# A hybrid RWKV-7 decoder block: the recurrence in chunks of 64 with all chunks batched, in place of chunks of 128 one after another

## The chip, the core and the metric

The kernel runs on one core of a Trainium2 chip. The metric is device time in microseconds (us) of one launch. Work is spread over engines that run their own instruction streams in a fixed order and meet at semaphores: TensorE (PE, matrix products into PSUM), VectorE (DVE), ScalarE (ACT), GpSimd (POOL) and SyncE (SP), whose queue issues most loads and stores.

## The reference

One decoder block over 512 tokens, width 2048, all in float32. What the change touches is the RWKV-7 mixer: 16 heads of 64 channels, each with a 64x64 state that runs through the 512 tokens.

```python
def _wkv7_scan(r, w, k, v, a, b):
    def step(S, inp):
        r_t, w_t, k_t, v_t, a_t, b_t = inp
        sa = jnp.einsum('bhvk,bhk->bhv', S, a_t)
        S = S * w_t[:, :, None, :] + sa[..., None] * b_t[:, :, None, :] + v_t[..., None] * k_t[:, :, None, :]
        y = jnp.einsum('bhvk,bhk->bhv', S, r_t)
        return S, y
...
    y = _wkv7_scan(r_h, decay, k_h, v_h, -kk, kk * a_h)
    # group norm of y per head, + bonus, * gate
...
    mix = jnp.concatenate([y_rwkv, y_pool], axis=-1) @ w_out[l]
    x = x + gt1 * mix
    x = x + gt2 * _conv_ffn(h, w_up[l], conv_w[l], conv_b[l], w_down[l])
```

Ahead of the scan stand the adaLN product, an RMS norm and the input projection `w_in`; beside it a causal pooling mixer; behind it the output projection and a gated MLP with a causal convolution of width 3.

## The kernel before

Activations lie channels by tokens, 128 channels on the partitions. Large products run in float32r with weights and activations split into a high and a low part, three matmuls each (`mm3`, L120 to L122); the recurrence's small products are plain float32.

The heads are handled as eight pairs, two heads on 128 partitions. For each pair:

- `stage_a` (L366) makes decay, key, value and the keys `bt`, `kt`, the queries `ar` (a removal part and a reading part), the scores of `bt` against the removal part (L417, masked at L420 into `nt`), and inverts the 16x16 diagonal blocks of (I - nt), through DRAM, on DVE (L435, L437). It ends with the bonus `bv`.
- `stage_b` (L466) doubles the inverse: from 16 to 32 with 32x32 products (L474, L483), from 32 to 64 (L496 to L508), and from 64 to 128 (L514 to L519). The result is `y1`, `y2`.
- `stage_c` (L523) walks through four chunks of 128 tokens, one after another. Each chunk transposes v, bt and kt (L532, copied by ACT at L534), makes three blocks of scores (L539, L541) and masks them (L542), multiplies the state and the values into R (L547, L550, copied at L553), applies the inverse (L556, L557, copied at L559 as U), forms the next state `sbd` (L562, L564, L573) and three sums of the output y (L578, L580, L582). A group norm with two 128x128 products (L590, L594), the gate (L602, L603) and a store to DRAM follow.

Around it, `win_pair` (21 tiles of input projection, spilled to DRAM) and `ada_rest` (192 adaLN products on DVE at L351, each with a 256 KB load) stand in the program at ordinary priority. The recurrence stands under `hp()`, a high priority. A scheduler orders each engine's stream at build time by priority and by its own estimate of readiness; on the chip the orders are fixed. `stage_c` of one pair is followed by `stage_b` of the next; `stage_a` of the next comes before them.

PSUM has eight banks: two for `mm`, two for `pa`, two joined as `pb`, one `y`, one `ch`.

A matmul with 64 rows contracted or 64 columns of weights occupies a part of the 128x128 array. The trace writes that as rows*columns (64*128, 128*64, 64*64, 32*32).

Of the kernel before, what the change touches and what calls it, by code (L numbers as in the profile page):

```python
# [9 lines left out]
F32 = mybir.dt.float32  # L10
# [6 lines left out]
P = 128  # L17
T = 512
# [4 lines left out]
NC = 4  # L23
WC = 512
# [31 lines left out]
def block_kernel(ctx, tc, a, out, stop=None, dbg=None):  # L56
# [18 lines left out]
    masks = tp.tile([P, 4, P], F32, tag="masks", name="masks")  # L75
    nc.sync.dma_start(masks, a["mask4"][:, :, :])
    mlev = tp.tile([P, 2, 64], F32, tag="mlev", name="mlev")
    nc.sync.dma_start(mlev, a["mlev"][:, :, :])
    scanm = tp.tile([P, NC, 129], F32, tag="scanm", name="scanm")
# [236 lines left out]
    def btile():  # L316

        return psa.tile([P, 2, T], F32, tag="pb", name="pb")

    def ctile(tag):  # L320
        return psa.tile([P, T], F32, tag=tag, name=tag)
# [11 lines left out]
    y1 = ra.tile([P, 8, 64], F32, tag="y1", name="y1")  # L333
    G.memset(y1[64:128], 0.0)
# [22 lines left out]
    def ch(t):  # L357
        return t[:, :].rearrange("p (c t) -> p c t", c=NC)
# [7 lines left out]
    def stage_a(p, rkv):  # L366
# [10 lines left out]
        sg = ra.tile([P, NC, 129], F32, tag="sg", name="sg", bufs=2)  # L377
        V.memset(sg[:, :, 0:1], 0.0)
        S.activation(sg[:, :, 1:129], ch(psw), AF.Sigmoid, bias=col("w0", p))
        al = ring("al")  # L380
        S.activation(al, psal, AF.Sigmoid, bias=col("a0", p))
        cs = ra.tile([P, NC, 129], F32, tag="sg", name="cs", bufs=2)
        V.tensor_tensor_scan(cs[:, :, :].rearrange("p c t -> p (c t)"), scanm[:, :, :].rearrange("p c t -> p (c t)"),
                             sg[:, :, :].rearrange("p c t -> p (c t)"), 0.0, op0=ALU.mult, op1=ALU.add)
        mid = ra.tile([P, NC, 1], F32, tag="mid", name="mid", bufs=2)
        V.tensor_copy(mid, cs[:, :, 64:65])
        V.tensor_sub(cs, cs, mid[:, :, :].to_broadcast([P, NC, 129]))
        ep = ra.tile([P, NC, 129], F32, tag="ep", name="ep")
        S.activation(ep, cs, AF.Exp, scale=-Q)
        em = ra.tile([P, NC, 129], F32, tag="em", name="em")  # L390
        S.activation(em, cs, AF.Exp, scale=Q)
        fdec = q.fdec = ra.tile([P, NC - 1, 1], F32, tag="fdec", name="fdec", bufs=2)
        V.tensor_mul(fdec, ep[:, 0 : NC - 1, 128:129], em[:, 1:NC, 0:1])
# [5 lines left out]
        PE.matmul(psn, bones, sq, start=True, stop=True)  # L399
        inv = ring("inv")  # L400
# [4 lines left out]
        ar = q.ar = ra.tile([P, NC, 2, P], F32, tag="ar", name="ar", bufs=2)  # L405
        V.scalar_tensor_tensor(ar[:, :, 0, :], ch(inv), -1.0, ep[:, :, 0:128], op0=ALU.mult, op1=ALU.mult)
        bt = q.bt = ra.tile([P, T], F32, tag="bt", name="bt", bufs=2)
        V.tensor_mul(bt, inv, al)
        V.tensor_mul(ch(bt), ch(bt), em[:, :, 1:129])
# [9 lines left out]
        for h in range(2):  # L419
            V.tensor_mul(ntv[:, h, :, :], ch(pss[h]), masks[:, 0:1, :].to_broadcast([P, NC, P]))  # L420
# [846 lines left out]
```

## Time and profile before

| | |
|---|---|
| runs | 2365.44, 2365.26, 2360.84 us; median 2365.26 |
| span of the profiled execution | 2365.6 us |
| granted TensorE clock, mean | 0.989 |
| PE busy, over the span | 2259.0 us, 95% |
| DVE, ACT, POOL busy | 1637.7, 1066.4, 126.2 us |
| DMA moved | 483.06 MB, mean 204 GB/s |

The profile is one execution. Busy time is the union of an engine's instructions. A group's row gives line, engine, operation, output and inputs, shapes, count, busy time, mean length of one in ns, idle time ahead of it and what ended that. A float32 matmul shows as two instructions of the same line. Matmuls overlap in their pipeline, and their ends are modelled, so the distance from start to start is what one costs, not its length.

### The profile page before, as it was taken

What the parts mean: (1) busy time and instruction counts of PE and PEld (TensorE: products, weight loads), DVE (VectorE), ACT (ScalarE), POOL (GpSimd) and SP (SyncE); (2) the same over time, 40 slices, a digit from 0 to 9 for tenths busy, and PEclk for the clock granted to TensorE, in tenths of its full rate; (3) what the DMA queues carried; (4) which work ended last, traced back from release to release, by engine and by line L of the source; (5) the groups of instructions that cost most, each with busy time, mean ns of one, the idle gap of its engine ahead of it and who ended that gap; (6) DMA issues with size and microseconds to landing.
All of it is one profiled execution on the core that took longest, in us unless ns stands there. A gap on an engine that the chain in (4) does not pass through costs nothing.

```text
span 2365.6 us, 42857 instructions
## 1 busy us (share of the span) xinstructions
PE 2259.0 (95%) x17122; PEld 1965.8 (83%) x17122; DVE 1637.7 (69%) x2591; ACT 1066.4 (45%) x1499; POOL 126.2 (5%) x185
## 2 busy tenths in 40 slices
PE   3879999999999999999999999999999999999997
PEld 2656666666666789999999999999999888888897
DVE  6987687777684456788888877777777645353354
ACT  3235253445433345665555555555555522233353
POOL 0000000000000000010101000000000000110000
PEclk9999999999999999999999999999999999999999
DMA  9976556566672756598888877777776767663464
GB/s 345 339 232 184 164 157 175 153 179 188 172 207 74 242 190 191 169 284 246 231 245 234 237 212 199 197 198 199 199 197 185 237 212 272 228 211 117 123 183 160
DMA packets 226234, 483.06 MB, mean 204 GB/s; under 512 B 74545, under 2 KB 79601, under 8 KB 217841
## 3 DMA queue, kind: packets, MB, share of 16 engines
q1 hardware_dynamic: 206114, 413.21, 54.5%
q0 software_dynamic: 18864, 66.07, 13.6%
q8 instruction: 134, 2.20, 0.4%
q10 hardware_dynamic: 1056, 1.05, 0.1%
q14 instruction: 66, 0.54, 0.1%
HBM read 441.70 MB, written 38.54 MB: 203 GB/s over the span
## 4 chain that ended last, share of the span: by engine, by line
PE 57%; issue 8%; DVE 1%; DMA 1%; ACT 1%; POOL 0%; POOLq 0%; DVEq 0%; ACTq 0%
PE b L122 18%; PE b L120 18%; PE b L121 18%; DMA wrow<-wup 1%; PE mm L122 1%; PE mm L121 1%; PE mm L120 1%; PE pb L122 0%; PE pa L122 0%; PE pa L120 0%; PE pa L121 0%; PE pb L120 0%; PE pb L121 0%; ACT x L787 0%; PE pa L298 0%
## 5 line engine op out<-in xcount | busy, mean ns | idle before, releaser
L122 PE MATMUL b<-t,ulo 128*128 128x256 f32 x1408 | 397.2, 282 | 0.0
L120 PE MATMUL b<-t,uhi 128*128 128x256 f32 x1408 | 396.8, 282 | 0.0
L121 PE MATMUL b<-t,uhi 128*128 128x256 f32 x1408 | 396.7, 282 | 0.0
L122 PE MATMUL b<-act,ulo 128*128 128x512 f32 (+1 forms) x880 | 308.0, 350 | 0.0
L121 PE MATMUL b<-act,uhi 128*128 128x512 f32 (+1 forms) x880 | 307.8, 350 | 0.0
L120 PE MATMUL b<-act,uhi 128*128 128x512 f32 (+1 forms) x880 | 307.7, 350 | 0.0
L120 PE MATMUL b<-y,uhi 128*128 128x256 f32 x1056 | 297.4, 282 | 2.7 <-ACT uhi L854 2.7
L122 PE MATMUL b<-y,ulo 128*128 128x256 f32 x1056 | 297.3, 282 | 0.5 <-DVE ulo L856 0.5
L121 PE MATMUL b<-y,uhi 128*128 128x256 f32 x1056 | 297.1, 281 | 0.0
L856 DVE TENSOR_TENSOR ulo<-wd,uhi 128x1024 fp32r<-128x1024 f32 (+1 forms) x120 | 136.3, 1136 | 217.9 <-ACT uhi L854 213.0
L113 ACT CAST whi<-wraw 128x512 fp32r<-128x512 f32 x236 | 145.5, 620 | 274.7 <-PE mm L121 115.3
L120 PEld LDWEIGHTS b<-t,uhi 128*128 128x128 f32 x1408 | 266.9, 190 | 0.0
L122 PEld LDWEIGHTS b<-t,ulo 128*128 128x128 f32 x1408 | 266.9, 190 | 0.0
L121 PEld LDWEIGHTS b<-t,uhi 128*128 128x128 f32 x1408 | 266.8, 190 | 0.0
L854 ACT CAST uhi<-wquart 128x1024 fp32r<-128x1024 f32 x156 | 164.0, 1052 | 202.6 <-PE b L121 176.2
L854 ACT CAST uhi<-wd 128x1024 fp32r<-128x1024 f32 (+1 forms) x120 | 117.6, 980 | 293.2 <-PE b L121 291.1
L856 DVE TENSOR_TENSOR ulo<-wquart,uhi 128x1024 fp32r<-128x1024 f32 x156 | 190.9, 1224 | 72.0 <-ACT uhi L854 72.0
L115 DVE TENSOR_TENSOR wlo<-wraw,whi 128x512 fp32r<-128x512 f32 x236 | 161.1, 688 | 100.3 <-ACT whi L113 92.6
L854 ACT CAST uhi<-r 128x1024 fp32r<-128x1024 f32 x132 | 138.8, 1051 | 163.2 <-PE b L121 161.3
L856 DVE TENSOR_TENSOR ulo<-r,uhi 128x1024 fp32r<-128x1024 f32 x132 | 161.3, 1222 | 61.9 <-ACT uhi L854 61.9
L120 PEld LDWEIGHTS b<-y,uhi 128*128 128x128 f32 x1056 | 199.6, 189 | 3.1 <-ACT uhi L854 3.1
L122 PEld LDWEIGHTS b<-y,ulo 128*128 128x128 f32 x1056 | 199.3, 189 | 0.9 <-DVE ulo L856 0.9
(314 smaller groups left out, 4719.0 us busy)
## 6 DMA issues: line engine op xcount, KB each, us to landing
wquart<-wup SPq DMA_DIRECT2D x176, 512.0 KB, 4.8
wa<-ada SPq DMA_DIRECT2D x48, 1024.0 KB, 6.9
war<-ada SPq DMA_DIRECT2D x192, 256.0 KB, 3.4
wd<-wdn SPq DMA_DIRECT2D x80, 512.0 KB, 3.8
wraw<-win SPq DMA_DIRECT2D x140, 256.0 KB, 4.1
wraw<-wout SPq DMA_DIRECT2D x96, 256.0 KB, 3.5
wquart<-wup POOLq DMA_DIRECT2D x44, 512.0 KB, 7.5
r<-wup SPq DMA_DIRECT2D x44, 512.0 KB, 4.6
```

Of the source, the lines that this page charges most:

```text
L113: S.copy(hi, raw)
L115: eng.tensor_tensor(lo, raw, hi[:, :].bitcast(F32), op=ALU.subtract)
L120: PE.matmul(ps, wh, xh, start=start, stop=False, skip_group_check=more)
L121: PE.matmul(ps, wh, xl, start=False, stop=False, skip_group_check=more)
L122: return PE.matmul(ps, wl, xh, start=False, stop=stop, skip_group_check=more)
L854: S.copy(hi[:, 0:n], src)
L856: lo_of[0] = V.tensor_tensor(lo[:, 0:n], src, hi[:, 0:n].bitcast(F32), op=ALU.subtract)
```

## The change

The recurrence runs in eight chunks of 64 tokens. The two chunks of a former chunk of 128 lie on the two halves of the partitions (index e), the two heads on the two halves of the channels (index h). The inverse is doubled up to 64 only. All products of a pair that need no state are made for all eight chunks together: scores, W = T A and U0 = T L V, the transition matrix `gd` of each chunk, the state's input, and the parts of the output that need no state. Six steps then carry the state from chunk to chunk, each a 128x128 by 128x64 matmul and one DVE operation that scales and adds; fourteen products with the states complete the output. The PSUM banks `y` and `ch` become one double tile `py`; the group norm and the gate use `pa`. The mask table shrinks from four 128x128 masks to two of 128x64. The remaining lines of the diff change sizes and names alike.

```diff
+L = 64
+NL = T // L
...
-    masks = tp.tile([P, 4, P], F32, tag="masks", name="masks")
+    masks = tp.tile([P, 2, L], F32, tag="masks", name="masks")
...
-    sbd = [ra.tile([P, P], F32, tag=f"sbd{i}", name=f"sbd{i}") for i in range(2)]
-    for t in sbd:
-        G.memset(t, 0.0)
+    gd = ra.tile([P, NL, P], F32, tag="gd", name="gd")
+    G.memset(gd, 0.0)
...
+        sb = q.sb = ra.tile([P, 8, 3, L], F32, tag="sb", name="sb", bufs=2)
         pss = [atile() for h in range(2)]
-        for c in range(NC):
-            for h in range(2):
-                PE.matmul(pss[h][:, c * P : (c + 1) * P], bt[HS[h], c * P : (c + 1) * P], ar[HS[h], c, 0, :],
-                          start=True, stop=True)
+        scores([pss[h] for h in range(2)], bt, ar)
...
+    def scores(banks, keys, ar):
+        for c in range(NC):
+            for e in range(2):
+                for h in range(2):
+                    j = 2 * c + e
+                    PE.matmul(banks[h][HS[e], c * 2 * L : (c + 1) * 2 * L], keys[HS[h], jl(j)], ar[HS[h], :, j, :],
+                              start=True, stop=True)
...
+    def to_rows(src, dst, eng):
+        ps = atile()
+        for c in range(NC):
+            PE.transpose(ps[:, c * P : (c + 1) * P], src(c), ident)
+        eng(dst, ps[:, :].rearrange("p (c h d) -> p h c d", c=NC, h=2))
...
     def stage_b(p, q):
+        pk = btile()
+        scores([pk[:, h, :] for h in range(2)], kt, ar)
+        V.tensor_mul(sk, pk[:, :, :].rearrange("p h (c i t) -> p (h c) i t", c=NC, i=2),
+                     masks[:, None, :, :].to_broadcast([P, 8, 2, L]))
+        to_rows(lambda c: v[:, c * P : (c + 1) * P], by_head(tok[:, 0, :, :]), S.copy)
+        to_rows(lambda c: ar[:, 0, 2 * c : 2 * c + 2, :].rearrange("p e t -> p (e t)"), by_head(rw[:, :, 0, :]), S.copy)
+        to_rows(lambda c: bt[:, c * P : (c + 1) * P], by_head(sb[:, :, 2, :]), S.copy)
+        to_rows(lambda c: kt[:, c * P : (c + 1) * P], by_head(tok[:, 1, :, :]), S.copy)
+        pl = atile()
+        for s in range(8):
+            for e in range(2):
+                PE.matmul(pl[HS[e], jl(s)], sk[HS[e], s, 0, :], tok[HS[e], 0, s, :], start=True, stop=True)
+        S.copy(rw[:, :, 1, :], r8(pl))
...
         for s in range(8):
-            o = slice(s * 64, s * 64 + 64)
-            PE.matmul(pX[0:64, o], Y[0:64, s, :], Tm[0:64, s, :], start=True, stop=True)
-            PE.matmul(pY[64:128, o], Tm[64:128, s, :], Y[64:128, s, :], start=True, stop=True)
-            PE.matmul(pY[0:64, o], Tm[0:64, s, :], Y[0:64, s, :], start=True, stop=True)
...
+            for e in range(2):
+                PE.matmul(pY[HS[e], jl(s)], Tm[HS[e], s, :], Y[HS[e], s, :], start=True, stop=True)
+        V.tensor_add(nt, Y, r8(pY))
...
     def stage_c(p, q):
-        for c in range(NC):
...
+        items = [(c, e, h, 2 * c + e, 4 * h + c) for c in range(NC) for e in range(2) for h in range(2)]
+        for c, e, h, j, s in items:
+            PE.matmul(pt[HS[e], h, c * 2 * L : (c + 1) * 2 * L], sb[HS[e], s, 0, :], rw[HS[e], s, :, :], start=True,
+                      stop=True)
+        for h, eng in enumerate((S.copy, V.tensor_copy)):
+            eng(rw[:, 4 * h : 4 * h + 4, :, :], pt[:, h, :].rearrange("p (s i d) -> p s i d", s=4, i=2))
+        pg = btile()
+        for c, e, h, j, s in items:
+            PE.matmul(pg[HS[h], e, jl(c)], rw[HS[e], s, 0, :], sb[HS[e], s, 2, :], start=c == 0, stop=True,
+                      skip_group_check=True)
...
+        py = btile("py")
...
+        for h in range(2):
+            V.tensor_tensor(gd[HS[h], :, HS[h]].rearrange("p (c e) k -> p e c k", e=2),
...
+        V.tensor_tensor(hs.rearrange("p (c e) d -> p e c d", e=2), pg[:, :, hi].rearrange("p e (c d) -> p e c d", c=NC),
...
+        for j in range(1, NL - 1):
+            o = pg[:, j % 2, jl(j // 2)]
+            PE.matmul(o, gd[:, j, :], hs[:, j - 1, :], start=True, stop=True)
+            V.scalar_tensor_tensor(hs[:, j, :], o, fdec[:, j, :], hs[:, j, :], op0=ALU.mult, op1=ALU.add)
+        for c, e, h, j, s in items:
+            if j:
+                PE.matmul(py[HS[h], e, jl(NC + c)], hs[HS[h], j - 1, :], ar[HS[h], 1, j, :], start=False, stop=True,
+                          skip_group_check=True)
...
-        pyc = ctile("y")
+        pyc = atile()
...
-        pv = ctile("ch")
+        pv = atile()
```

Two batches for the state's input and three for the output have the same form as the transition's, with other operands, and are left out above.

More of the change, by code (lines that the diff above doesn't have):

```diff
@@ L492, in stage_b @@
         pt = btile()
-        pT, pX, pY = pt[:, 0, :], pt[:, 1, :], pt[:, 0, :]
+        pT, pY = pt[:, 0, :], pt[:, 1, :]
         for s in range(8):
-            for h in range(2):
-                PE.matmul(pT[HS[h], s * 64 : s * 64 + 64], nt[HS[h], s, HS[h]], X[HS[h], s, :], start=True, stop=True)
+            for e in range(2):
+                PE.matmul(pT[HS[e], jl(s)], nt[HS[e], s, :], X[HS[e], s, :], start=True, stop=True)
         Tm = ra.tile([P, 8, 64], F32, tag="Tm", name="Tm")
@@ L507, in stage_b @@
-        V.tensor_add(y2[64:128], Y[64:128], r8(pY)[64:128])
-        V.tensor_add(y1[0:64], Y[0:64], r8(pY)[0:64])
-        pt = btile()
-        pT, pY = pt[:, 0, :], pt[:, 1, :]
-        for s in range(8):
-            PE.matmul(pT[64:128, s * 64 : s * 64 + 64], nt[0:64, s, 64:128], x5[:, s, :], start=True, stop=True)
-        Tm = ra.tile([P, 8, 64], F32, tag="Tm", name="Tm6")
-        S.copy(Tm[64:128], r8(pT)[64:128])
-        for s in range(8):
-            PE.matmul(pY[0:64, s * 64 : s * 64 + 64], Tm[64:128, s, :], y2[64:128, s, :], start=True, stop=True)
```

177 lines of the change are left out of this document (72 added, 105 removed).

## The prediction

> **What bounds the kernel now.** I read the page first, then the busy time by stretches, the waits of TensorE (PE), its timeline, and the groups by line.
>
> ```profile
> span 2365.6 us, 42857 instructions
> PE 2259.0 (95%) x17122; PEld 1965.8 (83%) x17122; DVE 1637.7 (69%) x2591; ACT 1066.4 (45%) x1499; POOL 126.2 (5%) x185
> ...
> PE 57%; issue 8%; DVE 1%; DMA 1%; ACT 1%; POOL 0%; POOLq 0%; DVEq 0%; ACTq 0%
> ```
>
> PE is busy 95% of the span and the chain that ended last is made of its instructions. The eight pairs of the recurrence are one stretch of that:
>
> ```profile
> core 0: us, PE busy (x) PEld busy (x) DVE busy (x) ACT busy (x) POOL busy (x), PEclk, DMA share, GB/s
> 0.00:178.00 178.00, 117.86 (x447) 89.87 (x448) 149.80 (x228) 58.40 (x90) 2.66 (x13) 0.95 0.87 305
> 178.00:751.00 573.00, 549.86 (x5356) 380.75 (x5355) 423.40 (x1092) 249.34 (x380) 0.00 (x0) 0.99 0.59 167
> 751.00:1000.00 249.00, 242.68 (x1517) 218.35 (x1518) 144.74 (x222) 123.68 (x204) 15.36 (x28) 0.99 0.60 189
> ```
>
> Between 178 and 751 us PE sits idle 573.00 - 549.86 = 23.1 us and no more, at a clock of 0.99. The recurrence runs at high priority and the input projections of later pairs (the `mm` matmuls, L120 to L122) fill its waits. So the state's sequence as such costs little now: what its waits leave is used. What the change is worth is what it takes from PE's own instruction stream, and whether PE gets new waits. DVE is busy 423.4 of 573 us, 74%.
>
> What PE pays for small matmuls stands in the timeline (start us, us, engine, line, operation):
>
> ```profile
> 315.24 1.16 PE L417 MATMUL pa<-ar,bt 64*128 64x128 f32 x16
> 316.24 0.39 PE L539 MATMUL pb<-ar,bt 64*128 64x128 f32 x4
> 316.46 0.60 PE L541 MATMUL pb<-ar,kt 64*128 64x256 f32 x4
> ...
> 361.83 0.75 PE L474 MATMUL pb<-x,nt 32*32 32x32 f32 x64
> 362.51 1.12 PE L399 MATMUL pa<-sq,hmat 128*128 128x512 f32 x2
> ...
> 369.48 0.39 PE L122 MATMUL mm<-ah,wlo 128*128 128x512 f32 x1
> 369.80 1.15 PE L496 MATMUL pb<-xy,nt 64*64 64x64 f32 x32
> 370.88 0.50 PE L120 MATMUL mm<-ah,whi 128*128 128x512 f32 x1
> 371.22 0.40 PE L121 MATMUL mm<-al,whi 128*128 128x512 f32 x1
> 371.46 0.40 PE L122 MATMUL mm<-ah,wlo 128*128 128x512 f32 x1
> ...
> 382.24 0.33 PE L532 MATMUL pa<-cmat,v 128*128 128x128 f32 x1
> ...
> 382.87 0.48 PE L120 MATMUL mm<-ah,whi 128*128 128x512 f32 x1
> ...
> 383.51 1.14 PE L518 MATMUL pb<-y,Tm 64*64 64x64 f32 x16
> 384.59 0.50 PE L122 MATMUL mm<-ah,wlo 128*128 128x512 f32 x1
> ```
>
> Starts, not durations, give the rate. An f32 matmul is two passes (L518 issues 8, the row says x16). L518 puts all into one 64x64 corner of the array: 16 passes in 384.59 - 383.51 = 1.08 us. L496 alternates two opposite corners: 32 passes in 370.88 - 369.80 = 1.08 us, two at a time. L539, which follows L417 in the same array shape, alternates the two row halves: 4 passes of 128 columns in 0.22 us, **0.11 us a matmul, two at a time**; at 64 columns I take half, 0.055, at 256 double, 0.22 (estimates from that row). L474 has four 32x32 tiles: 64 passes in 0.68 us. The six one-pass transposes from 382.24 to 382.87 take 0.105 each. Changing the array's shape costs too: from 369.48 to 371.22 are 1.74 us, less two `mm` matmuls at 0.235 (371.22 to 371.46) is 1.27, less 16 x 0.055 = 0.88 leaves 0.39 for two changes, **0.2 us a change**.
>
> **The change, part by part.** First PE, per pair, at these prices. Removed or replaced: L417 8 x 0.11 = 0.88; L539 0.88; L541 8 x 0.22 = 1.76; L496 16 x 0.055 = 0.88; L501 to L503, 16 in the fuller corner x 0.11 = 1.76; L514 and L518, one corner, 16 x 0.11 = 1.76; 12 transposes 1.26; L547 and L578 12 x 0.11 = 1.32; L550, L556, L557 32 x 0.055 = 1.76; L562, L564 12 x 0.055 = 0.66; L580, L582 16 x 0.11 = 1.76. Sum 14.7. In the order of the kernel before, 11 of 32 pairs of L539 and 15 of 32 of L541 are torn apart, so each half runs alone: (11 x 0.11 + 15 x 0.22) / 8 = 0.6 more. Together 15.3 us.
>
> Added, per pair: two sets of scores, 32 matmuls of 128 columns over all four corners; 16 transposes 1.68; TLV's product, the level-16 product and the Y product, 48 over two opposite corners x 0.055 = 2.64; W and U0, 16 of 128 columns over two corners, 1.76; six batches of 16 at 64 columns over all four corners (transition, two for the input, W's part of y, two more for y); six 128x128 state steps x 0.11 = 0.66; 14 output products x 0.055 = 0.77.
>
> Four corners at a time appear nowhere in the trace. Bounds: four at a time (as L474's tiles are) gives 32 x 0.055 + 96 x 0.0275 = 4.4 us; two at a time 8.8; one at a time 17.6. I take four: L539 shows the two row halves sharing columns at once, L496 both diagonal corners, L474 four tiles; and each order runs through the corners in turn with a row half to a PSUM bank. Sum then 4.4 + 7.5 = 11.9, that is 3.4 us less a pair, **-27 us** for eight.
>
> The Trainium skill, TensorEngine Tiling (Array Packing), Tiling Modes, agrees: 64x64 makes four independent tiles, and a change of mode drains the array. Another page, TensorE: Matmul & The Clock Gate, Part 3, speaks against: it says that matmuls start strictly in the program's order. By that rule a matmul's second pass would hold the next corner's first, and the sum would be the one of two at a time. The trace contradicts it in the rows of L501 to L503 below.
>
> ```profile
> 372.65 0.27 PE L502 MATMUL pb<-xy,Tm 64*64 64x64 f32 x1
> 372.71 0.22 PE L503 MATMUL pb<-xy,Tm 64*64 64x64 f32 x1
> 372.76 0.22 PE L502 MATMUL pb<-xy,Tm 64*64 64x64 f32 x1
> 372.76 0.28 PE L501 MATMUL pb<-Tm,xy 64*64 64x64 f32 x2
> ```
>
> The program's order is 501, 502, 503, 501, 502; here the second round's L502 in one corner starts at 372.65, ahead of that round's L501 in the other at 372.76. Corners queue for themselves.
>
> Second, shape changes. Counted in the static order from the first scores to the last gate product: 400 before, 271 after, since chunk by chunk went 64x128, 128x64, 128x128 and back, and the batches are nearly all 64x64. 129 x 0.2 = **-26 us**. The number of switches between filler and small work hardly moves (286 and 280), so this is all inside the small runs.
>
> Third, DVE and ACT, per pair:
>
> ```profile
> L351 DVE SCALAR_TENSOR_TENSOR war<-war,cq 128x512 f32<-128x512 f32 x186 | 125.1, 684 | 20.9 <-DMA war<-ada 20.5
> L115 DVE TENSOR_TENSOR wlo<-wraw,whi 128x512 fp32r<-128x512 f32 x95 | 64.6, 686 | 25.3 <-ACT whi L113 22.6 <-PE mm L122 1.6 <-DMA wraw<-win 0.7
> L542 DVE TENSOR_TENSOR L<-pb,masks 128x768 f32<-128x768 f32 x32 | 30.6, 956 | 4.7 <-PE pb L541 4.1
> L351 DVE DVE_READ_ACCUMULATOR war<-war,cq 128x1 f32 x186 | 15.0, 81 | 0.0
> L559 DVE COPY U<-ch 128x128 f32<-128x128 f32 x32 | 9.3, 292 | 25.2 <-PE ch L557 22.7 <-issue 2.1
> L573 DVE SCALAR_TENSOR_TENSOR sbd<-ch,fdec,sf 64x64 f32<-64x64 f32 x32 | 9.0, 282 | 4.1 <-PE ch L564 3.6
> L507 DVE TENSOR_TENSOR y<-xy,pb 64x512 f32<-64x512 f32 x8 | 5.5, 691 | 0.1
> ...
> L534 ACT COPY tok<-pa 128x384 f32<-128x384 f32 x32 | 15.4, 480 | 62.1 <-PE pa L532 34.2 <-PE ch L564 27.7
> L553 ACT COPY R<-ch 128x128 f32<-128x128 f32 x32 | 8.5, 266 | 51.6 <-PE ch L550 51.5
> L569 ACT ACTIVATE sf<-sbd,fdec 128x128 f32<-128x128 f32 x16 | 6.4, 403 | 2.8 <-DVE sbd L573 1.3 <-DVE sbd L575 1.1
> L588 ACT COPY y<-y 128x512 f32<-128x512 f32 x8 | 4.7, 586 | 6.6 <-PE y L582 6.6
> ```
>
> DVE loses 4 x 0.956 + 4 x 0.292 + 6 state writes at L573's 0.282 + 3 adds at L507's 0.691 = 8.8 us. It gains one mask product of 1024 columns (0.956 x 1024 / 768 = 1.27, an estimate), the W copy, two transition adds, the input scaling, W's part of y and the Y add, six of 512 columns at 0.69, and six state steps at 0.28: 7.1. ACT loses 4 x 0.48 + 4 x 0.266 + 2 x 0.403 + two copies near L588's 0.586 = 5.0 and gains six copies of 512 columns, 3.5. Both run beside PE, so this is no term; it says that DVE asks for 423 - 14 = 409 us of a stretch of some 521, 79% and not 74%.
>
> Fourth, waits that take the place of others. Behind the W and U0 products PE stands at the transition batch until ACT and DVE have copied them, about 0.1 + 0.59 + 0.1; ahead of it stand 13 of the next pair's scores, 13 x 0.055 = 0.7: 0.1 to 0.2 short. The group norm's matmuls lose part of their four `mm` matmuls of cover to scores that run fast, and their PSUM tiles now come from the two that the next pair's transposes use: 0.1 to 0.3. For a state step the state write of today shows the hand-overs:
>
> ```profile
> 395.72 0.29 PE L564 MATMUL ch<-U,tok 128*64 128x64 f32 x4
> 396.06 0.28 DVE L573 SCALAR_TENSOR_TENSOR sbd<-ch,fdec,sf 64x64 f32<-64x64 f32 x1 [0.23 <-PE ch L564]
> 396.48 0.29 DVE L573 SCALAR_TENSOR_TENSOR sbd<-ch,fdec,sf 64x64 f32<-64x64 f32 x1
> 396.82 0.43 PE L578 MATMUL y<-ar,sbd 128*64 128x128 f32 x2
> ```
>
> PE's end at 396.01 to DVE's start and DVE's end at 396.77 to PE's start are 0.05 each, so a step of matmul (0.27 to its end), DVE (0.28) and next matmul takes some 0.65. PE's cover in each step is its matmul, two output products, two shape changes and 2 to 5 `mm` matmuls, 1.1 to 1.8 us; in DVE's order stands mostly one adaLN product (L351, 0.684 + 0.081) between two steps, so DVE's round is 1.05. It just fits. I take half a us a pair, **+4 us**; the bounds are -23 (the idle time of today gone) and the second rival's price.
>
> At nothing: the smaller mask load (64 KB for 256) in the DMA-filled head, at 305 GB/s at most 0.6 us; the larger memset of the transition tile, on POOL, which the stretch shows idle and which has until the first pair's third stage. No load, store or queue entry of the recurrence is added or moved past another on SP.
>
> Sum against the profiled execution: 2365.6 - 27 - 26 + 4 = 2316.6; that execution stands 0.3 us above the runs' median of 2365.26. **Forecast 2317 us.**
>
> **Rivals.**
> Two corners at a time: 4.4 us more a pair, +35: 2352. For it: no row shows four 64x64 corners; a bank or a read path could admit two. Against it: L474 and the sharing shown by L539. The order rule of the Trainium skill cited above (TensorE: Matmul & The Clock Gate, Part 3) would end here too.
>
> The state steps set the pace (slower): if two DVE instructions stand ahead of each step, an L351 and an L115, 0.765 + 0.686 = 1.45 us are added to each of 48 steps, 70 us: 2317 + 70 - 4 = 2383. It turns slower than before once a step loses more than 49 / 48 = 1.0 us. For it: DVE would be 79% full in a fixed order, and L351 already waits 20.5 us for its loads, which then hold up a step. Against it: in that order most steps have one between them, and PE's filler stands there.
>
> Corners one at a time: 17.6 - 4.4 = 13.2 a pair, +106: 2423. L496 and L539 speak against it.
>
> Nothing moves: the stretch is set by DVE or by the adaLN loads, and PE's gain becomes idle: 2365. Against it: 23.1 us idle on PE, 150 on DVE, a DMA share of 0.59.
>
> **How the numbers follow.** Forecast 62%, two corners 22%, late steps 9%, nothing moves 4%, one corner 3%. The forecast's own range is 2294 (idle time gone) to 2340. To leave out no more than two in ten it has to reach past the two-corner case with a little extra waiting: 2294 to 2360. A measurement of this kernel tells some 0.2%, 4.7 us, from no change. Faster by more than that: the first case nearly whole and most of the second, 0.83; within it 0.05, nothing moves and the edge of two corners; slower 0.12, late steps and one corner.
>
> **What would show it.** Right: in the timeline a batch of 16 matmuls at 64 columns over four corners (x32) followed after about 0.5 to 0.6 us by the next, scores x32 after about 1 us; the eight pairs over by about 700 us; PE's idle time there near 25 us. Two corners: those batches take 0.9 us, scores 1.8. Late steps: waits of the state matmuls on DVE's step above 20 us in the list of waits. Wrong altogether: PE's idle time above 60 us, or batches slower than L496's.

## The result and the profile after

The changed kernel takes 2378.3 us, the median of ten runs (2365.4 to 2387.4); the kernel before took 2363.2 on the same chip. The ratio is 1.0062 with a 95% interval of 1.0040 to 1.0083: slower by some 15 us, where 2317 was forecast. The profiled execution took 2386.2 us, one of the slowest of the ten; from the fastest (2365.4 us) to the slowest the granted clock goes from 0.984 to 0.974, and 1% of the span is all of the 22 us between them. Its page and its core's clock:

```profile
span 2384.5 us, 44692 instructions
PE 2248.9 (94%) x18114; PEld 1976.6 (83%) x18114; DVE 1623.7 (68%) x2567; ACT 1051.7 (44%) x1451; POOL 126.1 (5%) x183
...
core 0: 2384.5 us, clock 0.973
```

A span splits into three: PE's idle time (span less PE's busy time), what the clock took (the records show the clock at 1 or at one half, so half of the time that PE was busy at half clock), and the rest, PE's work as it would be at full clock. Before: 2365.6 - 2259.0 = 106.6 idle; 19.6 clock; 2239.4 work. After: 135.6, 54.0 and 2195.0. So **PE's work fell by 44.4 us; its idle time rose by 29.0 and the clock's share by 34.4**. That makes +19.0, the difference of the two spans within rounding. The forecast had -53, +4 and nothing. Eight runs below have the same matmuls as the changed kernel, ordered otherwise; their work comes out at 2196 to 2203, so some 8 us in this column are scatter.

The eight pairs now end at 757 us (750 before), and what stands behind them is 12 us longer, because PE has 34 more matmuls left there (after, then before):

```profile
757.00:2384.50 1627.50, 1604.42 (x11358) 1503.13 (x11356) 1068.90 (x1282) 761.17 (x1035) 123.40 (x172) 0.99 0.70 205
750.00:2365.60 1615.60, 1592.32 (x11324) 1495.38 (x11323) 1064.46 (x1272) 759.64 (x1030) 123.55 (x172) 0.99 0.70 206
```

So the pairs did less of the filler in more time. Their stretch in the windows view (columns as in the prediction), and the waits of PE there:

```profile
178.00:765.00 587.00, 531.51 (x6325) 386.46 (x6326) 406.45 (x1059) 236.34 (x332) 0.00 (x0) 0.92 0.58 161
```
```profile
PE py L592 <- DVE ar L583: 10.0, 7, 3.5
PE pb L521 <- issue: 8.0, 4, 2.3
PE pa L455 <- DVE sb L414: 7.5, 7, 1.8
PE pb L588 <- DVE rw L574: 7.0, 7, 1.5
PE pb L557 <- DVE rw L552: 3.6, 6, 0.7
```

PE idles 55.5 us there (23.1 before), at a clock of 0.92 (0.99). The waits (total us, times, longest): four of these five rows come about once a pair and name DVE: the Y addition (L583), the masks of the next pair's scores (L414), the scaled input (L574), the copy of W (L552). DVE's own waits in that stretch:

```profile
DVE war L347 <- DMA war<-ada: 39.3, 30, 3.6
DVE rw L589 <- PE pb L588: 35.6, 31, 2.2
```

The first is the adaLN product waiting for its load, 20.5 us before. One pair shows how these fit together. PE's timeline, then DVE's:

```profile
391.18 0.69 PE L557 MATMUL pb<-sb,rw 64*64 64x64 f32 x32 [0.59 <-DVE rw L552]
391.70 0.34 PE L560 MATMUL pb<-rw,sb 64*64 64x64 f32 x10
...
394.94 1.12 PE L455 MATMUL pa<-k,hmat 128*128 128x512 f32 x2 [1.16 <-DVE sb L414]
...
396.28 0.65 PE L580 MATMUL py<-sk,tok 64*64 64x64 f32 x32
398.17 0.43 PE L588 MATMUL pb<-rw,gd 128*128 128x64 f32 x2 [1.25 <-DVE rw L574]
...
398.96 0.40 PE L122 MATMUL mm<-ah,whi 128*128 128x512 f32 x1
399.19 0.39 PE L123 MATMUL mm<-al,whi 128*128 128x512 f32 x1
400.58 0.48 PE L592 MATMUL py<-ar,rw 64*64 64x64 f32 x2 [1.00 <-DVE ar L583]
...
411.19 0.63 PE L123 MATMUL mm<-al,whi 128*128 128x512 f32 x1
411.61 0.63 PE L124 MATMUL mm<-ah,wlo 128*128 128x512 f32 x1
```
```profile
390.44 0.69 DVE L552 COPY rw<-pb 128x512 f32<-128x512 f32 x1 [0.24 <-ACT rw L552]
391.05 0.68 DVE L347 SCALAR_TENSOR_TENSOR war<-war,cq 128x512 f32<-128x512 f32 x1
391.65 0.08 DVE L347 DVE_READ_ACCUMULATOR war<-war,cq 128x1 f32 x1
393.58 0.69 DVE L347 SCALAR_TENSOR_TENSOR war<-war,cq 128x512 f32<-128x512 f32 x1 [1.84 <-DMA war<-ada]
394.20 0.08 DVE L347 DVE_READ_ACCUMULATOR war<-war,cq 128x1 f32 x1
394.20 1.28 DVE L414 TENSOR_TENSOR sb<-pa,masks 128x512 f32<-128x512 f32 x2
395.40 0.68 DVE L347 SCALAR_TENSOR_TENSOR war<-war,cq 128x512 f32<-128x512 f32 x1
396.00 0.08 DVE L347 DVE_READ_ACCUMULATOR war<-war,cq 128x1 f32 x1
396.00 1.39 DVE L570 TENSOR_TENSOR gd<-pb,cmat 64x512 f32<-64x512 f32 x2
397.42 0.69 DVE L574 TENSOR_TENSOR rw<-pb,fdec 128x512 f32<-128x512 f32 x1
```

L557's 32 passes, over all four corners, run from 391.18 to 391.70: 0.52 us, 16 ns a pass. The input and half of y follow at the same rate and PE is through by some 393.8. DVE, in its fixed order, waits at 391.73 for an adaLN load, has the products, masks, transition and input one after another behind it, and ends L574 at 398.11; only then can the first state step start (398.17). PE idles 0.59, 1.16, 1.25 and 1.00 us in ten. What that does to the clock stands in windows of 3.4 us:

```profile
393.40:396.80 3.40, 2.24 (x73) 1.33 (x65) 3.21 (x8) 0.00 (x0) 0.00 (x0) 1.00 0.59 160
396.80:400.20 3.40, 1.54 (x15) 0.90 (x6) 3.37 (x8) 0.00 (x0) 0.00 (x0) 1.00 0.27 41
400.20:403.60 3.40, 3.02 (x14) 2.45 (x14) 1.51 (x5) 0.00 (x0) 0.00 (x0) 0.51 1.02 243
403.60:407.00 3.40, 3.40 (x15) 2.58 (x15) 1.77 (x5) 0.62 (x1) 0.00 (x0) 0.50 0.55 152
```

After a window in which PE was busy 1.54 of 3.40 us the clock is half, here up to 413.9. An `mm` matmul then takes 411.61 - 411.19 = 0.42 us from start to start, against 399.19 - 398.96 = 0.23: the state steps and the filler behind the waits run at half speed.

### The profile page after: what moved, and what is told of

Its sections match the earlier page's. It is cut to its first block, busy times and chain, and to the rows that moved or that the text cites. A ratio compares the mean times of both kernels' runs of the same rounds, so it can differ in the third digit from the quotient of the medians.

```text
span 2384.5 us, 44692 instructions
## 1 busy us (share of the span) xinstructions
PE 2248.9 (94%) x18114; PEld 1976.6 (83%) x18114; DVE 1623.7 (68%) x2567; ACT 1051.7 (44%) x1451; POOL 126.1 (5%) x183
## 3 DMA queue, kind: packets, MB, share of 16 engines
q0 software_dynamic: 18864, 66.07, 13.7%
## 4 chain that ended last, share of the span: by engine, by line
PE 50%; issue 8%; DVE 1%; ACT 1%; DMA 0%; POOL 0%; POOLq 0%; DVEq 0%; ACTq 0%
PE b L124 17%; PE b L122 17%; PE b L123 17%; ACT x L796 0%; DMA wrow<-wup 0%; DVE xr L793 0%; DVE ulo L865 0%; ACT t L801 0%; DVE t L905 0%; POOL x L1149 0%; DVE wlo L117 0%; DVE u L894 0%; ACT uhi L863 0%; DVE acc L746 0%; POOLq L1270 0%
## 5 line engine op out<-in xcount | busy, mean ns | idle before, releaser
L122 PE MATMUL mm<-ah,whi 128*128 128x512 f32 x464 | 196.9, 424 | 6.2 <-ACT upad L267 5.5
```

Of the source, the lines that this page charges most:

```text
L122: PE.matmul(ps, wh, xh, start=start, stop=False, skip_group_check=more)
```

## The experiments

Two theories to begin with. **A**: DVE comes late, with adaLN products and the waits for their loads between the batches' copies, PE idles, and the clock halves after such windows. **B**: the small matmuls themselves count as little activity, or cost more than they seem. Each run is timed against the kernel before on the same chip. Three columns split the span of its profiled execution as above; the last gives PE's idle time and the time at half clock from 178 us to the last pair's end.

| run | us, median (range) | ratio to before [95%] | idle | clock | work | in the pairs: idle, half clock |
|---|---|---|---|---|---|---|
| before | 2365.3 (2360.8 to 2365.4) | | 106.6 | 19.6 | 2239.4 | 23, 17 |
| changed | 2378.3 (2365.4 to 2387.4) | 1.0062 [1.0040, 1.0083] | 135.6 | 54.0 | 2195.0 | 55, 89 |
| e1_ada_behind | 2360.7 (2350.2 to 2367.5) | 0.9986 [0.9962, 1.0010] | 127.4 | 30.3 | 2200.3 | 46, 34 |
| e2_after_no_ada | 2350.6 (2346.8 to 2364.5) | 0.9957 [0.9931, 0.9983] | 121.7 | 24.5 | 2199.7 | 41, 24 |
| e3_before_no_ada | 2360.4 (2359.0 to 2363.1) | 0.9987 [0.9970, 1.0004] | 105.0 | 14.5 | 2239.2 | 23, 10 |
| e4_two_corners | 2371.5 (2362.6 to 2381.8) | 1.0029 [1.0006, 1.0053] | 128.7 | 48.6 | 2202.9 | 48, 75 |
| e5_gd_on_act | 2383.3 (2370.4 to 2388.7) | 1.0077 [1.0055, 1.0098] | 133.5 | 42.5 | 2200.2 | 51, 65 |
| e6_ada_and_gd | 2359.7 (2354.0 to 2366.0) | 0.9981 [0.9966, 0.9996] | 124.9 | 34.6 | 2200.6 | 45, 55 |
| e7_ten_useless_matmuls | 2407.1 (2399.8 to 2411.2) | 1.0179 [1.0151, 1.0207] | 138.1 | 57.7 | 2213.6 | 58, 102 |
| e8_before_ada_behind | 2378.5 (2374.6 to 2381.8) | 1.0061 [1.0040, 1.0082] | 115.9 | 27.3 | 2235.9 | 34, 41 |
| g1_ada_outside_chain | 2392.4 (2381.6 to 2400.0) | 1.0114 [1.0069, 1.0159] | 148.1 | 42.9 | 2202.9 | 67, 63 |
| g3_zero_products_in_wait | 2388.9 (2381.4 to 2391.2) | 1.0103 [1.0075, 1.0132] | 131.8 | 44.7 | 2212.8 | 49, 65 |
| g4_before_ada_outside | 2408.8 (2399.6 to 2428.7) | 1.0204 [1.0151, 1.0257] | 137.4 | 23.9 | 2236.5 | 57, 31 |
| h1_ada_loads_pool_queue | 2414.3 (2410.7 to 2414.9) | 1.0212 [1.0195, 1.0229] | 162.5 | 52.7 | 2197.5 | 81, 102 |
| k1_no_ada_two_corners | 2344.6 (2342.6 to 2355.6) | 0.9935 [0.9913, 0.9956] | 118.2 | 24.5 | 2205.8 | 36, 27 |
| k2_filler_in_wait | 2388.1 (2384.3 to 2399.8) | 1.0114 [1.0084, 1.0144] | 142.9 | 59.3 | 2195.7 | 61, 99 |
| k3_ada_behind_filler | 2358.8 (2348.0 to 2368.8) | 0.9978 [0.9961, 0.9994] | 126.9 | 43.0 | 2197.1 | 45, 65 |
| k5_ada_20_a_pair | 2415.4 (2411.2 to 2420.9) | 1.0220 [1.0193, 1.0247] | 185.5 | 32.8 | 2198.0 | 47, 41 |
| k6_ada_14_a_pair | 2462.2 (2459.6 to 2465.7) | 1.0413 [1.0386, 1.0440] | 234.2 | 30.3 | 2199.1 | 43, 34 |
| k7_before_ada_14 | 2479.0 (2476.3 to 2483.2) | 1.0490 [1.0466, 1.0513] | 218.2 | 22.0 | 2236.7 | 28, 21 |

B falls by `e1_ada_behind` and `e2_after_no_ada` below: with the same small matmuls the half clock in the pairs goes from 89 us to 34 and 24. A fares better in kind than in number. The half-clock time fell into or below its range in five of the eight runs of the changed kernel for which it gave one. Its times came true for `e1_ada_behind`, `e3_before_no_ada` and `e4_two_corners` alone; the other eight lie above what it allowed.

Two limits hold for all rows. The split of a row is that of one execution. And nearly every edit also made the scheduler lay out DVE's order anew. Between DVE's copy of W and the first state step stand, over the eight pairs, 31 adaLN products in the changed kernel, 39 in `e5_gd_on_act`, 41 in `e7_ten_useless_matmuls`, 38 in `g3_zero_products_in_wait` and 43 in `k2_filler_in_wait`: these four put more of what A blames into the wait, and none is a clean test of its own edit. `e4_two_corners` and `k1_no_ada_two_corners` have the DVE order of the kernels that they are compared with.

### Does PE's work in the batches set the time?

`e4_two_corners`: the six batches, each in an order that takes two opposite corners first and then the other two, in place of all four in turn.

```diff
+        two = [i for d in range(2) for i in items if (i[1] ^ i[2]) == d]
...
-        for c, e, h, j, s in items:
+        for c, e, h, j, s in two:
```

> The changed kernel with the six batches over four corners reordered so that only two opposite corners alternate: 0.93 us a batch and not 0.5, PE passes +20 us over eight pairs. Theory A: the batches are cover that DVE needs anyway, so the time moves by at most +8 us and PE idle falls by 10 us or more; half-clock time falls to 50 to 85 us. If PE's passes set the pace: +20 us, 2395 to 2405. Theory B (packing itself trips the clock): half-clock time below 50 us.

PE's work is 7.9 us longer by the table, not 20: in the trace a batch follows the one before after 0.59 to 0.70 us (starts at 392.93, 393.63, 394.22), where the changed kernel shows 0.52 and 0.93 had been expected. The next batch begins in the two corners that are free. The time did not grow: 2371.5 against 2378.3. `k1_no_ada_two_corners` repeats it without the adaLN products:

> The changed kernel without the adaLN products (its second part of the modulation left at zero; 2350 us) and with six batches in the order that keeps only two corners busy (with the products that cost 9 us of PE work and no time). If PE's work in the pairs still sets the time once the products are gone: 2357 to 2362 us. If a chain through DVE and ACT sets it: 2346 to 2354 us.

6.1 us more work than `e2_after_no_ada`, and 2344.6 against 2350.6 us. In neither case is there a sign that PE's time in the batches reaches the end; but both steps are hardly larger than the intervals of the ratios, some 5 us each way.

### The adaLN products left out, in both kernels

```diff
+    G.memset(modq, 0.0)
...
-        ada_rest(min(28 * p, 192), min(28 * p + 28, 192))
```

> The changed kernel without the 192 adaLN products and their loads in the recurrence stretch (their part of the modulation is left at zero). Theory A: PE idle in the stretch at most 30 us, half-clock time at most 35 us, time 2315 to 2335. Theory B: half-clock time stays above 70 us, time above 2355.

> The kernel before without the same products and loads. Theory A: its waits were filled, so little is gained: PE idle 10 to 23 us, half-clock time about 17 us or less, time 2345 to 2363; the changed kernel without them is then the faster by 20 to 40 us. Theory B: the same for this kernel, but the changed one without them stays slower or equal.

Both edits leave the second part of the modulation at zero. The changed kernel gains 28 us, the kernel before 3. The two stretches, changed and before:

```profile
178.00:712.00 534.00, 493.17 (x6283) 359.01 (x6282) 299.55 (x676) 232.13 (x325) 0.00 (x0) 0.98 0.32 82
```
```profile
178.00:732.00 554.00, 530.62 (x5299) 364.02 (x5298) 312.85 (x706) 247.32 (x377) 0.00 (x0) 0.99 0.32 80
```

The changed kernel's pairs are over 20 us sooner, but PE still idles 40.8 us against 23.4. By the split, work is 39.5 us less, idle time 16.7 and the clock's share 10.0 more: of 40 us 13 arrive. With the products, the changed kernel was 15 us behind by the medians, without them it is 10 ahead. So the products and their loads are about half of the loss, and not all of it: A had expected 2315 to 2335 us here. Which part is the products' time on DVE and which their loads, these two runs don't separate.

### The same products elsewhere

`e1_ada_behind` queues a pair's products behind its last state step; `e8_before_ada_behind` is the same edit of the kernel before.

```diff
-            V.scalar_tensor_tensor(hs[:, j, :], o, fdec[:, j, :], hs[:, j, :], op0=ALU.mult, op1=ALU.add)
+            step = V.scalar_tensor_tensor(hs[:, j, :], o, fdec[:, j, :], hs[:, j, :], op0=ALU.mult, op1=ALU.add)
...
-        ada_rest(min(28 * p, 192), min(28 * p + 28, 192))
+        with tc.issue_after(step.ins):
+            ada_rest(min(28 * p, 192), min(28 * p + 28, 192))
```

> The changed kernel with one edit: each pair's adaLN products (DVE) are queued behind that pair's last state step; those that are late still reach into the next pair's third stage. Theory A (DVE comes late: adaLN products and their waits for loads stand between the batches' copies, PE idles, and the clock is halved after such windows): partly relieved, PE idle in the recurrence stretch 35 to 50 us (55.5 in the changed kernel), half-clock time there 40 to 80 us (89), time 2345 to 2370. Theory B (the small packed matmuls themselves count as little activity, the clock falls whatever DVE does): half-clock time stays 80 to 100 us, time 2370 to 2385.

> The kernel before with its adaLN products queued behind the last state write of each pair: the control of the same edit that took the changed kernel from 2378 to 2361 us. Theory A: the kernel before has no low-occupancy windows that this could remove (idle 23.1 us, half clock 17 us in the pairs' stretch, and without any adaLN products at all it took 2360), so 2357 to 2368 us. If the adaLN products cost either kernel alike, whatever the recurrence: 2345 to 2352 us.

The changed kernel gains 18 us, and the first pair alone gains more than that. Its stretch, changed kernel and then `e1_ada_behind`:

```profile
178.00:291.00 113.00, 98.45 (x955) 71.44 (x956) 74.16 (x198) 42.14 (x60) 0.00 (x0) 0.89 0.57 155
```
```profile
178.00:265.00 87.00, 80.55 (x919) 58.45 (x918) 57.85 (x143) 41.41 (x58) 0.00 (x0) 1.00 0.40 103
```

No product stands in the first pair any more, it ends 26 us sooner, and the clock stays at 1.00. From the second pair on nothing is gained (469 us against 466): the products had only moved to the next pair, where in DVE's order 5 to 7 of them stand between its copy of W and the first state step, where the changed kernel has 4 to 6 (second pair to seventh). The kernel before is slower by 15 us with the same edit, against both expectations; so its own arrangement was a good one for it.

`g1_ada_outside_chain` and `g4_before_ada_outside` also hold the next pair's third stage on DVE behind those products, so that none stands inside it:

```diff
-            step = stage_c(p, q)
+            with tc.issue_after(last.ins) if p else contextlib.nullcontext():
+                step = stage_c(p, q)
```

> The changed kernel with the 192 adaLN products in DVE's order outside the chain: those of a pair stand behind that pair's last state step, and the next pair's third stage stands behind them on DVE (in the first adaLN experiment they had only been moved back, so that 5 to 7 of them stood between the next pair's W copy and its first state step again; here none does). Loads and products are all there. Theory A (products with their loads' waits inside DVE's chain leave PE idle, and the clock halves after such windows): close to the kernel without any products (2350 us), 2345 to 2360 us, half clock in the pairs' stretch 15 to 40 us. If it is DVE's total work and not its place: 2362 to 2378 us.

> The kernel before with the same edit: a pair's adaLN products behind its last state write, and the next pair's third stage behind them on DVE. Theory A: its third stage is spread over four chunks with PE's filler between them and lost little to the products (2360 us without any), so nothing is to be gained: 2358 to 2375 us. If the place of the products costs both kernels alike: 2340 to 2350 us.

Both became slower, against both expectations. In the first, PE's waits moved to the weights' halves and to the inverse:

```profile
PE mm L123 <- ACT whi L116: 10.5, 6, 2.9
PE pb L535 <- DVE xy L526: 9.4, 7, 2.4
```

So A's narrow form, that the products cost only by standing between W and the state steps, falls: none stands there now. That they hold up whatever else stands behind them in DVE's order fits these waits, and is not shown by itself.

`k5_ada_20_a_pair`, `k6_ada_14_a_pair` and, on the kernel before, `k7_before_ada_14` put fewer products into the pairs and the rest behind the last:

```diff
-            ada_rest(min(28 * p, 192), min(28 * p + 28, 192))
+            ada_rest(14 * p, 14 * p + 14 if p + 1 < NP else 192)
```

> The changed kernel with 20 adaLN products queued behind the last state step of each of the pairs 0 to 6 in place of 28, and the other 52 behind the last pair, where DVE is idle half the time. If the number of products, with their late loads, in the pairs' stretch sets the loss: between 2361 us (28 a pair behind the step) and 2350 us (none at all), 2348 to 2358 us. If their number does not matter: 2358 to 2366 us.

> The same with 14 a pair and 94 behind the last pair. If the number in the stretch sets the loss: 2346 to 2356 us, no slower than with 20, unless the 94 products hold the output projection, which would show as a shorter pairs' stretch with PE idle behind it. If the number does not matter: 2358 to 2366 us.

> The kernel before with its adaLN products the same way, 14 a pair behind the last state write and 94 behind the last pair. Without any products it took 2360 us. If its cover hides them: 2357 to 2368 us, so the changed kernel arranged like this is the faster of the two. If both kernels lose alike to the products: 2345 to 2356 us.

All three lost time to something else, as this wait of PE in `k6_ada_14_a_pair` shows:

```profile
PE pa L300 <- DMA pw<-poolw: 108.7, 1, 108.7
```

The pooling mixer's weights use the same three buffers as the products, so their load stood behind the 94, and PE with it (107.8 us in `k7_before_ada_14`). At 20 a pair PE waits 56.2 us at the same line; there the trace names the sum on DVE behind the products (L677). These three say nothing of what fewer products would do to the whole time. The stretch of the pairs shortened little, from 733.6 to 731.8 us at 20 a pair and 725.4 at 14; without products it ended at 711.9. At 14 a pair no product stands between the copy of W and the first state step, and the pairs have 43 us of PE idle time and 34 us of half clock, near the 41 and 24 without any.

The five arrangements, side by side. The last column is the ratio of the changed kernel to the kernel before under the same edit, each first taken against the unedited kernel before on its own chip (intervals combined from the two):

| the products | before, us | changed, us | changed / before |
|---|---|---|---|
| where the scheduler put them | 2363.2 | 2378.3 | 1.0062 [1.0040, 1.0083] |
| behind the last state step | 2378.5 | 2360.7 | 0.9925 [0.989, 0.996] |
| outside the third stage | 2408.8 | 2392.4 | 0.991 [0.984, 0.998] |
| 14 a pair | 2479.0 | 2462.2 | 0.9927 [0.989, 0.996] |
| none | 2360.4 | 2350.6 | 0.9970 [0.994, 1.000] |

In four of five the changed kernel is ahead by 10 to 18 us; in the last of them the interval just reaches 1, and in the row of 14 a pair both kernels stand in the wait of 108 us. The row of the case is the one with all products in which the kernel before stands best, and there the gain is lost.

### The lateness itself

`h1_ada_loads_pool_queue` issues the products' loads from POOL's queue in place of SP's.

```diff
-            nc.sync.dma_start(wa, a["ada2"][kq, j, :, :])
+            nc.gpsimd.dma_start(wa, a["ada2"][kq, j, :, :])
```

> The changed kernel with the 192 adaLN loads issued from POOL's queue (idle in the pairs' stretch) in place of SP's, where they stand behind other waits in a fixed order. If SP's order makes the loads late and so holds DVE: DVE's wait for these loads falls from 39 us to under 20, PE idle in the stretch from 54.7 to 40 to 48, time 2355 to 2370 us. If the loads are late for lack of buffers or of DMA rate, or do not matter: wait above 30 us, 2373 to 2385 us.

It went the other way, its time outside both expectations; its waits of DVE and of PE:

```profile
DVE war L347 <- DMA war<-ada: 69.8, 55, 3.8
```
```profile
PE pb L521 <- DVE Tm L515: 24.4, 5, 6.9
PE pb L588 <- DVE rw L574: 14.3, 7, 3.5
```

DVE waits 30.5 us longer for these loads, PE idles 26.9 us more in the whole run, the time is 36 us longer, and PE's work is the same within 3 us. Later loads go with a later DVE and an idler PE, as A says. Why the loads issued from POOL come later was not followed up.

### Less on DVE, more on PE

`e5_gd_on_act` adds the identity of the transition on PE and copies the tile by ACT; `e6_ada_and_gd` is that on top of `e1_ada_behind`.

```diff
+        for e in range(2):
+            for h in range(2):
+                PE.matmul(pg[HS[h], e, lo].rearrange("p (c k) -> p c k", c=NC), ident[HS[e], HS[e]],
+                          ident[HS[e], None, HS[e]].to_broadcast([64, NC, L]), start=True, stop=False,
+                          skip_group_check=True)
...
-            V.tensor_tensor(gd[HS[h], :, HS[h]].rearrange("p (c e) k -> p e c k", e=2),
...
+            S.copy(gd[HS[h], :, HS[h]].rearrange("p (c e) k -> p e c k", e=2),
+                   pg[HS[h], :, lo].rearrange("p e (c k) -> p e c k", c=NC))
```

> The changed kernel, but the transition's identity is added on PE (four more 64x64 matmuls of 256 columns a pair, ahead of the transition batch, into the same tile) and the tile is copied into gd by two ACT copies in place of two DVE additions. Two DVE instructions of about 0.7 us less stand in DVE's chain between the W copy and the first state step; PE gets at most 4 x 0.22 = 0.9 us a pair more, 7 us in all. Theory A (DVE, late in its fixed order, leaves PE idle, and the granted clock halves after such stretches): idle on PE in the pairs' stretch falls from 54.7 to 40 to 50 us, time at half clock from 88.7 to 50 to 80, in all 2360 to 2376 us against 2378, although PE's work grows. Theory B (the small packed matmuls themselves count as little activity, DVE's place does not matter): 2378 to 2388 us, time at half clock unchanged within 10 us.

> Both edits: the adaLN products queued behind the last state step of a pair (alone 2360.7 us) and the transition copied by ACT with the identity added on PE. Theory A: both take DVE work from between PE's batches, so the gains add in part: idle in the pairs' stretch 30 to 42 us, half clock 15 to 34 us, 2340 to 2358 us, faster than the kernel before by 0.3 to 1%. Theory B: no better than the first edit alone, 2359 to 2368 us, PE's work being 4 to 7 us longer.

Two additions fewer on DVE, 1.4 us a pair, change nothing that can be measured: 2383.3 against 2378.3, 2359.7 against 2360.7; A's times for both were missed. In the first, eight more products stand in their place, 0.77 us each; in the second 33 for the 36 of `e1_ada_behind`, and there is no gain either.

### The clock

`e7_ten_useless_matmuls` and `g3_zero_products_in_wait` give PE work that is not needed: ten matmuls a pair ahead of W's part of y, and eight products with zero ahead of the first state step.

```diff
+        with tc.issue_after(last.ins):
+            for i in range(10):
+                PE.matmul(py[:, i % 2, :], H[15][0][:, 0:P], H[15][0], start=True, stop=True)
```
```diff
+        with tc.issue_after(last.ins):
+            for i in range(NZ):
+                for h in range(2):
+                    zero = PE.matmul(py[HS[h], i % 2, hi], noth, q.kt[:, 0 : NC * L], start=False, stop=False,
+                                     skip_group_check=True)
```

> The changed kernel with ten useless 128x128 by 512 float32r matmuls a pair (0.23 us each at full clock, 18 us in all), queued on PE between the state's input batches and W's part of y, where PE now waits for DVE; their result is overwritten. Theory A with the clock as the larger part: the stretch's low-occupancy windows around the transition disappear, time at half clock in the stretch falls from 88.7 to 30 to 55 us, idle from 54.7 to 35 to 48 us, and with 18 us more work on PE the whole still takes 2355 to 2372 us, no longer than the changed kernel's 2378. Theory B, or waits that merely move behind the added matmuls: half clock unchanged within 10 us, 2390 to 2400 us.

> The changed kernel with eight products with a zero matrix a pair (128x64 by 256 columns, float32, into the open sums of y, which they do not change), queued on PE where it waits for DVE ahead of the first state step; 4 x 0.44 = 1.8 us a pair, 14 us in all, nothing on DVE's chain waits for them. A test of the clock by itself. If windows with a low share of busy PE time halve the clock: PE idle in the stretch falls by 8 to 14 us, half clock from 88.7 to 40 to 70 us, and the time is shorter than the changed kernel's 2378 although PE does more: 2355 to 2374 us. If the clock does not follow PE's busy time: half clock unchanged within 10 us, time 2378 to 2390 us.

The first added 18.6 us of work and 29 us of time. Its place was wrong: the Y addition needs what now stood behind the ten, and DVE was late all the same. One line of its DVE timeline, with a wait of 4.61 us for a load:

```profile
273.01 0.69 DVE L347 SCALAR_TENSOR_TENSOR war<-war,cq 128x512 f32<-128x512 f32 x1 [4.61 <-DMA war<-ada]
```

The second, in the wait itself, added 17.8 us of work and no time to the stretch (it ended at 755.8 us, 757.1 without), but left some 20 more matmuls for behind it; the clock's share fell by 9.3 us and the granted clock there rose to 0.94:

```profile
178.00:757.00 579.00, 530.49 (x6419) 382.80 (x6417) 403.86 (x1053) 231.84 (x326) 0.00 (x0) 0.94 0.57 162
```

The clock followed as A says (median over its executions 0.980, against 0.978), but less was won back than the work cost: 2388.9 us, outside what A expected. `k2_filler_in_wait` and, on `e1_ada_behind`, `k3_ada_behind_filler` put needed work there, 12 matmuls of the next input projection in pairs 2 to 5:

```diff
+        if fill:
+            with tc.issue_after(last.ins):
+                last = fill()[-1]
...
-            PE.matmul(o, gd[:, j, :], hs[:, j - 1, :], start=True, stop=True)
+            with tc.issue_after(last.ins):
+                PE.matmul(o, gd[:, j, :], hs[:, j - 1, :], start=True, stop=True)
...
+                rest = win_groups(p + 2)
+                fill = next(rest) if p > 1 else None
```

> The changed kernel with 12 matmuls of the next input projection (2.7 us of work that has to be done anyway) put into PE's order ahead of the first state step, where PE waits for DVE, in pairs 2 to 5. If misplaced filler is the cause: idle falls by 6 to 9 us, half clock by 10 to 25 us, and time from 2378 to 2358 to 2371 us. If not: 2373 to 2384 us.

> The same filler in the same place, on the kernel with the adaLN products queued behind the last state step (2360.7 us alone). If misplaced filler is the cause: 2343 to 2355 us, faster than the kernel before by 0.4 to 0.9%. If not: 2357 to 2366 us.

2388.1 against 2378.3, above both expectations, and 2358.8 against 2360.7: no gain. PE's waits in `k2_filler_in_wait`:

```profile
PE py L596 <- DVE ar L586: 11.7, 5, 4.0
PE pa L396 <- ACT sq L394: 7.1, 4, 2.4
```

The filler is missing elsewhere: PE's wait at L396, 3.2 us in the changed kernel, is 7.1 here, and the one for the Y addition stays, with more products ahead of it. So moving filler into this wait did not help as it was done here; that its place plays no part is not shown.

## Why the prediction was wrong

**PE's work: right in kind, 10 to 20 us too large.** -27 for passes and -26 for shape changes, 53 us, against 44.4 in these two profiles (33 to 44 over all pairs of profiles with the same matmuls). Which of the two terms is short, no run separates. Four corners do run at once (16 ns a pass; L496's two gave 34), against which the rule of order in the Trainium skill, TensorE: Matmul & The Clock Gate, Part 3, had spoken. The rivals of two corners and of one are out.

**From PE's work to the time: the step that failed.** "What the change is worth is what it takes from PE's own instruction stream, and whether PE gets new waits": the forecast let all 53 us of work that it took out of PE's stream arrive in the time, and asked for new waits at three places only. Of the 44 us that were taken out none arrived. `e4_two_corners` and `k1_no_ada_two_corners` show that 8 and 6 us of work could be put back without a longer time.

**The waits, "+4 us": mis-sized.** The stretch's idle time rose by 32 us and the whole run's by 29. The prediction weighed the state steps and the copy of W each against an average cover, with DVE as "no term" because its instructions only grew from 74% to 79%. The sum of DVE's work was about right (406.5 us against 409). What counts is its order: in the pair shown, batches that took PE some 3 us end before DVE has finished what stands ahead of their copies, products with late loads among it. The L351 row with its 20.5 us of waiting was quoted, and used for the state steps only.

**The clock: no term at all.** The prediction read 0.99 and carried it over. It fell to 0.92 in the stretch and took 34 us more over the run, the largest single part of the loss; half clock comes behind windows with such waits. In the pair shown, 13.7 us at half clock (400.2 to 413.9) cost 6.9 us, the four waits ahead of them 4.0.

**The other terms put at nothing.** The mask load and the memset do not appear among PE's waits in the pairs, ACT only in small rows (3.2 us at L396 the largest). DVE does, as shown.

**The rivals.** Late DVE, at 9% and 2383 us, is what happened in time (2378) and in kind. Not in place: it was priced at the state steps, and its mark, over 20 us of waits of the state matmuls, shows 10.0 + 7.0. The waits lie ahead of the first step and at the next pair's masks, and half of the loss is the clock, so that its number came near is in part luck. "Nothing moves", PE's gain turned into idle time, came nearest to the mechanism at 4%.

**Its own signs.** The batches of 0.52 us were seen; pairs over by 700 us and idle time near 25 were not (757 and 55.5).

What stays open: why the scheduler's order suited the kernel before so well that every move of its products cost time, and what holds the changed kernel's pairs at 40.8 us of idle time without any product, which is the other half of the loss. More buffers for the loads, or a pool tile apart from them, were not tried. Of the versions that compute the whole block the best, `k3_ada_behind_filler` and `e6_ada_and_gd`, stand at 0.998 of the kernel before.

## What to carry to other kernels

An engine that is 95% busy does not promise that all of what is taken from its instructions arrives in the time. Ask at each batch which copy of another engine stands behind it and what stands ahead of that copy in that engine's fixed order, late loads included. Work that waits for no other engine (here a product with its own load) is not free filler in a fixed order. Price idle time twice: once as time, and once as the clock that is lost after it.

## What the hardware showed that was not expected

**The clock halves after windows that are partly busy.** The half clock comes in pieces of 3.41 us and multiples. Between 178 and 758 us of all 20 profiles, of the 3.41 us windows at full clock in which PE was busy (union of its matmuls) under 40%, 72 of 72 were followed by half clock; at 40 to 50%, 57 of 73; at 50 to 60%, 18 of 80; above that, 12 of 2855. The kernel before had 3 windows under 50%, the changed kernel 8. The Trainium skill, TensorE: Matmul & The Clock Gate, Part 1 (The HAM clock gate), gives the same window, 3413 ns, and has the clock halve after an idle one. Here PE was never idle for a whole window in the pair shown: 1.54 of 3.40 us of work did not keep the clock.

**Four 64x64 corners share the array fully in float32**: 16 ns a pass at 64 columns (L557); two corners take 34 (L496), one 67 (L518), both from the kernel before. A corner can run ahead of the program's order, as the prediction's rows of L501 to L503 show.
